# Row factors of two blocks from the transposed input, a ring of its own in the output projection, and later ties for the loads of h

## The chip, the cores and the metric

One core of a Trainium2 chip runs the kernel. TensorE (PE) multiplies matrices, with weight loads listed apart as PEld; VectorE (DVE), ScalarE (ACT) and GpSimd (POOL) work on vectors; SyncE (SP) issues all DMA transfers of this kernel, in the order of its queue. The metric is the device time of one execution in microseconds, as a median of several runs.

## What is computed

One step of a one-layer hybrid encoder over 2048 prompt rows and 32 sample rows of width 1024, all in float32. Cut to what matters here:

```python
def rmsnorm(x, g, eps=EPS):
    xf = x.astype(jnp.float32)
    y = xf * lax.rsqrt(jnp.mean(xf * xf, axis=-1, keepdims=True) + eps)
    return (y * g.astype(jnp.float32)).astype(x.dtype)
...
qa, ka, va, qb, kb, vb = split_proj(rmsnorm(hp, g_attn[i]), w_in[i])
oa = diff_attn_prompt(qa, ka, va, t5_table, lam)
ob = band_attn_prompt(qb, kb, vb, band_table[i])
hp = hp + merge(oa, ob, subln_g[i], out_norm_b[i], w_out[i], lam_init)
...
c = rmsnorm(h, g_mlp)
h = h + jnp.square(jax.nn.relu(c @ w_up)) @ w_down
return h + jax.nn.sigmoid(h @ w_ple_gate) * (p @ w_ple_proj)
```

A row of x (one token) thus gets a factor, 1 / sqrt(mean of its squares + eps), before the projection. A last rmsnorm gives y. Keys and values are outputs too.

## The kernel before

The tokens stand in four blocks of 512 columns (block 1 has the 32 sample rows as well), with features on the partitions: an operand is a tile of 128 partitions by 8 feature groups by 512 tokens. Each float32 operand is split into a high part (rounded, by an ACT copy) and a low part (the rest, by a subtraction on DVE or POOL), and each product is three matmuls: high by high, high by low, low by high (mm3, L267 to L269).

The stages, in the order of the program: preparation and projection of blocks 0 and 1 and their attention; preparation of blocks 2 and 3 (prep, woven with projections of group B); attention of group B; projections of group A for blocks 2 and 3 (proj_a), with onorm of blocks 0 and 1 beside them; the rest of the attention; the output projection of blocks 0 and 1; the MLP of these two; output projection of 2 and 3; then the MLP of blocks 2 and 3 as seven products over half blocks (uphase, dphase); the gates; the end.

A tile framework places the instructions. The program gives each a priority by its place, `tc.high_priority` can raise it ("lifted" does that for the preparation of blocks 2 and 3), and a model of the time (`schedule_with_timeline_sim=True`) then writes each engine's queue. An engine works through its queue in order, and waits with it. A buffer of a pool is given out again once all that read it have run.

What the change and the prediction speak of:

- prep: for each chunk of 256 tokens it loads x twice, as rows (xrows: two tiles of 128 tokens by 1024) and transposed (xcols: xt, one buffer in this stage). ACT squares the rows and sums them (L393), rsqrt makes the factor for 128x2 values, PE transposes it to a row of all partitions (rp, L397), ACT copies it out (rb, L401); then DVE multiplies xt by weight and factor (L405), and ACT and DVE split it into aH and aL (L235, L241).
- weave2 and ONP: while proj_a runs, onorm of block 0 is stepped at its yields 16 and 22, that of block 1 at 17 and 23. A first step loads group B's attention output (oraw), squares and sums it; a second makes the factor and stores it in rB.
- oload(1) and norms(0), beside the output projections of blocks 0 and 1: they load oraw, or tmp from hS, into the ring "tmp" of the pool wk, three buffers, which outproj uses as well for hd and tmp. When the pool is a Mix, oload and outproj load one tile ahead.
- dphase: products 3, 5, 7, 4, 2, 6, 1 in this order, each of 8 chunks (c) of two halves (k). A half needs a split piece of u (dx, four buffers) and of w_down (dw). After a product, DVE adds its result into h. Product 3 adds into block 3's h alone, product 5 into both.
- hstep (L1699 to L1703): in product 3, at chunks 0 to 3, POOL copies one column of dx into each of four h tiles (L1702), and SP then loads these h tiles from hS: the copy ties the load to that place. The h tiles lie where uphase had its temporary tiles.
- gates: the gates of blocks 0 and 1 are woven into dphase; they split their own h (hH, hL) and load w_ple_gate.

Of the kernel before, what the change touches and what calls it, by code (L numbers as in the profile page):

```python
# [12 lines left out]
F32 = mybir.dt.float32  # L13
F32R = mybir.dt.float32r
AF = mybir.ActivationFunctionType
ALU = mybir.AluOpType
# [3 lines left out]
P = 128  # L20
D = 1024
# [9 lines left out]
EPS = 1e-6  # L31
# [13 lines left out]
HALVES = [(0, 1), (2, 3)]  # L45
# [68 lines left out]
OW = 1  # L114
# [1 line left out]
JA0 = [(0, 1), (2, 3, 8)]  # L116
JA1 = [(4, 5), (6, 7)]
JB = [(0, 1), (2, 3, 8), (4, 5), (6, 7)]
ONP = (16, 1, 6)
ONQ = (8, 1, 1)  # L120
PW = 256
GL = 3
# [20 lines left out]
def weave(main, side, step, i=0, n=1):  # L143
    for _ in main:
        if i % step == 0:
            for _ in range(n):
                next(side, None)
        i += 1
    drain(side)
# [47 lines left out]
class Kern:  # L197
# [183 lines left out]

    def prep(self, b, acts, pp, mm, tag, xs=()):
        nc = self.nc
        aH, aL = acts[b]
        xs = list(xs)
        for c0, n in [(0, 256), (256, 256)] + ([(512, SS)] if b == 1 else []):
            m = min(n, P)
            nt = n // m
            x = [xs.pop(0) if xs else self.xrows(b, c0 + P * i, m, pp) for i in range(nt)]
            xt = xs.pop(0) if xs else self.xcols(b, c0, n, pp)  # L390
            st = pp.tile([P, 2], F32, tag="st", name="st")
            for i in range(nt):
                nc.scalar.activation(x[i][:m], x[i][:m], AF.Square, accum_out=st[:m, i : i + 1])  # L393
            r = self.rsqrt(pp, st[:m, :nt], nt, 1.0 / D, EPS, nc.vector, "r1", m)
            rp = mm.tile([P, 512], F32, tag=tag, name="rp")
            for i in range(nt):
                nc.tensor.transpose(rp[:, m * i : m * i + m], r[:, i : i + 1].broadcast_to([m, P]), self.ident[:m, :m])  # L397
            rb = rp
            if b:
                rb = pp.tile([P, 256], F32, tag="rb", name="rb")  # L400
                nc.scalar.activation(rb[:, :n], rp[:, :n], AF.Copy)  # L401
            yield
            for k0 in range(0, 8, 2):
                for k in range(k0, k0 + 2):
                    nc.vector.scalar_tensor_tensor(  # L405
                        xt[:, k, :n], xt[:, k, :n], self.g_attn[:, k : k + 1], rb[:, :n], op0=ALU.mult, op1=ALU.mult
                    )
                sl = (slice(None), slice(k0, k0 + 2))
                self.split(aH[sl + (slice(c0, c0 + n),)], aL[sl + (slice(c0, c0 + n),)], xt[sl + (slice(0, n),)], "act", "dve")
                yield  # L410

    def ktok(self, b):
        if b != 1:
# [782 lines left out]
    def dphase(self, h, pool, md, step):  # L1196
        nc = self.nc
        def wrow(q, c):
            i, j = int(q[0]) - 1, int(q[1]) - 1
            r = pool.tile([P, 2, 512], F32, tag="wd", bufs=6, name="wd")  # L1200
            self.dma(r.rearrange("p a b -> p (a b)"), self.a["w_down"][8 * j + c, i])
            return r

        def operands(m, sq, so, c):
            ws = [wrow(q, c) for q in sq]
            u = self.rawp.tile([P, 2, 512], F32, bufs=self.nraw, name="ut")
            self.dma(u, self.uS[:, m - 1, 2 * c : 2 * c + 2])
# [12 lines left out]
        plan = [  # L1220
            (3, ("11",), add, (("12", add), ("22", add))),
            (5, ("11", "12"), add, (("11", sub), ("12", add))),
            (7, ("12", "22"), sub, (("11", add),)),
            (4, ("22",), add, (("11", add), ("21", add))),
            (2, ("21", "22"), add, (("21", add), ("22", sub))),
            (6, ("21", "11"), sub, (("22", add),)),
            (1, ("11", "22"), add, (("11", add), ("22", add))),
        ]
        for m, sq, so, outs in plan:
            ps = [md.tile([P, 512], F32, tag="mm", name="dp") for _ in range(4)]  # L1230
            for c in range(8):
                for k, (w, x) in enumerate(operands(m, sq, so, c)):
                    if m == 3 and k == 0:
                        step(c, x)
                    for d in range(4):
                        sl = slice(P * d, P * d + P)
                        self.mm3(
                            ps[d], [(w[:, 0, sl], w[:, 1, sl], x[:, 0], x[:, 1])],
                            start=c + k == 0, stop=c == 7 and k == 1,
                        )  # L1240
                if c < 7:
                    yield
            adds = [(d, q, op) for d in range(4) for q, op in outs]
            if m == 1:
                adds.sort(key=lambda x: x[1])
            for d, q, op in adds:
                i, t = int(q[0]) - 1, int(q[1]) - 1
                hv = h[2 + t][4 * i + d]
                nc.vector.tensor_tensor(hv, hv, ps[d], op=op)
            yield  # L1250
# [231 lines left out]
    def run(self):  # L1482
        tc, nc, a = self.tc, self.nc, self.a
        with ExitStack() as top:

            def opened(stack, name, bufs, space=None, side="left"):
                kw = {} if space is None else {"space": space}
                return stack.enter_context(
                    tc.tile_pool(name=name, bufs=bufs, side=side, reuse_waits="tile", **kw)
                )  # L1490
# [7 lines left out]
            mm = opened(psx, "mm", MM, PSUM)  # L1498
# [7 lines left out]
            sg = opened(s12, "sg", 2)  # L1506
            wr = (self.wp, "wr", 3)
            self.rawp = Rings(wr, wr, wr, (opened(s12, "rw", 1), "wr", 1))
            acts = {b: self.actpair() for b in HALVES[0]}
            with ExitStack() as x:  # L1510
                self.nx = 2
                pp = opened(x, "pp0", 3, side="right")
                spare = opened(x, "w4", 1, side="right")
                xs = [self.xrows(0, P * i, P, pp) for i in range(2)]
# [6 lines left out]
                wk = opened(x, "setup", 1, side="right")  # L1521
# [18 lines left out]
            pp = opened(ppx, "pp", 1)  # L1540
# [10 lines left out]
            one, rest = (0,), (1, 2, 3)  # L1551
# [3 lines left out]
            def lifted(gen):  # L1555
                while True:
                    with tc.high_priority(tc.tile_snap_priority() - mark):
                        done = next(gen, self) is self
                    if done:
                        return  # L1560
                    yield

            acts[2] = self.actpair()
            weave(self.proj((1,), 1, acts, sg, mm, vs=(), gs=rest), lifted(self.prep(2, acts, pp, mm, "mm")), 1, 0, 2)
            acts[3] = self.actpair()
            bx = ExitStack()
            bp = opened(bx, "b", 1, side="right")
            for js in JB[: len(JB) // 2]:
                self.attn_b(js, bp, ps_s, ps_t, ps_o)
            prep = lifted(self.prep(3, acts, pp, mm, "mm"))  # L1570
            weave(self.proj((2,), 1, acts, sg, mm, vs=(), gs=rest), prep, 1, 0, 2)
            ppx.close()
            self.vr = Rings(vr)
# [18 lines left out]
            oa = {}  # L1592
# [8 lines left out]
            wk = opened(sq_, "wk", 1)  # L1601
            acc, cn, st = {}, {}, {}
            def norms(b, act, ps):
                r = self.colnorm(acc[b][0], b, 1.0 / D, wk, ps, "mm", None)
                yield
                yield from self.cnorm(b, wk, act, cn, r)

            acc = {b: [] for b in range(4)}
            with ExitStack() as x:
                oq = Sized(opened(x, "oq", 2), BLK, True)  # L1610
                weave(self.outproj(0, wk, oa[0], mm, acc[0]), self.oload(1, wk, oq, oa), 1, 0, OW)
                weave(self.outproj(1, wk, oa[1], mm, acc[1]), norms(0, actq, mm), 1, 1)
            hq = opened(sq_, "hq", 1)
            uq = Sized(opened(sq_, "uq", 10), BLK)
# [7 lines left out]
            def hmove(b, h, load, ds=range(8)):  # L1622
                for d in ds:
                    x, y = h[d][:, : BN[b]], self.hS[:, d, T0[b] : T0[b] + BN[b]]
                    self.dma(*((x, y) if load else (y, x)))
                return h
# [69 lines left out]
            h = {b: hh.tile([P, 8, 512], F32, tag="h", name="h") for b in HALVES[1]}  # L1696
            h = {b: [t[:, d] for d in range(8)] for b, t in h.items()}

            def hstep(c, x):  # L1699
                for b in HALVES[1] if c < 4 else ():  # L1700
                    for d in (2 * c, 2 * c + 1):
                        nc.gpsimd.tensor_copy(h[b][d][:, :1], x[:, 0, :1].bitcast(F32))  # L1702
                    hmove(b, h[b], True, range(2 * c, 2 * c + 2))  # L1703

            fk = opened(top, "fk", 1)
            udx, gqx = ExitStack(), ExitStack()
# [90 lines left out]
```

## Time and profile before

| | |
|---|---|
| median of 3 runs | 2965.36 us (2957.69 to 2965.66) |
| the profiled execution's own time | 2963.89 us |
| its span, first to last instruction | 2962.1 us |
| TensorE's mean granted clock | 0.993 |
| PE busy | 2899.6 us |
| DVE, ACT, POOL busy | 1754.8, 1753.6, 1349.1 us |

In the profile, a row of a group or a timeline gives engine, source line, operation, `out<-in` by the program's names and the shape. "[8.40 <-ACT dx L235]" says that the engine was idle for 8.40 us before the instruction, and that ACT's instruction on dx at line 235 ended it. A row of waits gives the total in us, the number of times and the longest. Lines 235, 241, 220 and 230 belong to helpers, so the tile's name tells where one is. A landing time tells when a DMA's data was there.

### The profile page before, as it was taken

The page shows a single profiled execution, that of the slowest core. Times are in us where ns is not written, and L with a number is a line of the kernel's source. Part 1 is how long each engine was busy: PE and PEld are TensorE (multiplying, and loading weights), DVE is VectorE, ACT ScalarE, POOL GpSimd, SP SyncE. Part 2 cuts the span into 40 slices and gives each one's busy share as a digit, 9 for nine tenths or more (in the row PEclk, how much of TensorE's full clock was granted, in tenths as well). Part 3 has the DMA queues.
Part 4 walks back from the last instruction along what each step waited for, and adds up shares of the span by engine and source line. Part 5 has one row for each costly group of instructions (what it writes and reads, how often), then busy time and mean ns, then how long its engine had stood idle before and what let it go on. Part 6 is the DMA issues. An engine that isn't in the chain of part 4 may idle for free.

```text
span 2962.1 us, 49251 instructions
## 1 busy us (share of the span) xinstructions
PE 2899.6 (98%) x17041; PEld 2560.4 (86%) x17041; DVE 1754.8 (59%) x3930; ACT 1753.6 (59%) x3729; POOL 1349.1 (46%) x1863
## 2 busy tenths in 40 slices
PE   8999999999999999999999999999999989999998
PEld 7899888998889888888899999889788868888886
DVE  6566664444565543565766564447665656766965
ACT  5566666665666665766777675443545445555554
POOL 4675664333355555655455455440855533133000
PEclk9999999999999999999999999999999999999999
DMA  9975578766677544544743433566443495756811
GB/s 347 328 249 198 192 259 271 219 210 207 226 252 225 192 159 157 166 154 151 240 138 123 148 109 120 183 205 199 164 149 139 146 342 191 267 194 202 265 64 57
DMA packets 299785, 578.28 MB, mean 195 GB/s; under 512 B 34672, under 2 KB 132080, under 8 KB 299536
## 3 DMA queue, kind: packets, MB, share of 16 engines
q1 hardware_dynamic: 299536, 575.13, 58.3%
q8 instruction: 135, 2.21, 0.3%
q14 instruction: 114, 0.93, 0.1%
HBM read 443.81 MB, written 131.22 MB: 194 GB/s over the span
## 4 chain that ended last, share of the span: by engine, by line
PE 89%; DMA 5%; DVE 3%; ACT 2%; issue 1%; POOL 1%; SPq 0%; ACTq 0%; DVEq 0%; POOLq 0%
PE s L607 4%; PE ups L269 4%; PE ups L267 4%; PE ups L268 4%; PE dps L267 4%; PE dps L268 4%; PE dps L269 4%; PE qps L267 4%; PE qps L269 4%; PE qps L268 4%; PE xps L269 3%; PE xps L268 3%; PE xps L267 3%; PE dp L267 3%; PE dp L269 3%; PE dp L268 3%
## 5 line engine op out<-in xcount | busy, mean ns | idle before, releaser
L230 POOL TENSOR_TENSOR wl<-wr,wh 128x256 fp32r<-128x256 f32 x888 | 667.8, 783 | 703.2 <-ACT wh L235 583.2
L235 ACT ACTIVATE wh<-wr 128x1024 fp32r<-128x1024 f32 x258 | 272.5, 1056 | 214.4 <-PE dps L268 43.5
L267 PE MATMUL ups<-cH,wh 128*128 128x272 f32 (+1 forms) x768 | 249.9, 326 | 2.3 <-ACT cH L235 1.2
L267 PE MATMUL dps<-uh,wh 128*128 128x272 f32 (+1 forms) x768 | 250.5, 328 | 1.5 <-DVE h L1001 1.1
L269 PE MATMUL ups<-cH,wl 128*128 128x272 f32 (+1 forms) x768 | 249.7, 326 | 0.6 <-DVE wl L241 0.6
L268 PE MATMUL ups<-cL,wh 128*128 128x272 f32 (+1 forms) x768 | 249.6, 325 | 0.0
L268 PE MATMUL dps<-ul,wh 128*128 128x272 f32 (+1 forms) x768 | 248.7, 324 | 0.2 <-DVE ul L241 0.2
L269 PE MATMUL dps<-uh,wl 128*128 128x272 f32 (+1 forms) x768 | 247.9, 324 | 0.0
L267 PE MATMUL qps<-aH,wh 128*128 128x512 f32 (+3 forms) x640 | 228.8, 357 | 6.6 <-DVE qk L487 3.0
L269 PE MATMUL qps<-aH,wl 128*128 128x512 f32 (+3 forms) x640 | 227.4, 355 | 0.0
L268 PE MATMUL qps<-aL,wh 128*128 128x512 f32 (+3 forms) x640 | 226.8, 354 | 0.0
L268 PE MATMUL dp<-dx,dw 128*128 128x512 f32 x448 | 177.9, 397 | 0.0
L267 PE MATMUL dp<-dx,dw 128*128 128x512 f32 x448 | 168.1, 399 | 9.1 <-ACT dx L235 9.1
L269 PE MATMUL dp<-dx,dw 128*128 128x512 f32 x448 | 174.9, 397 | 0.0
L607 PE MATMUL s<-ka,q 128*128 128x512 f32 (+3 forms) x640 | 173.3, 368 | 0.5 <-DVE nm L616 0.4
L788 DVE CUSTOM_DVE_ANT_0 eb<-sb,bb 128x320 f32<-128x320 f32 (+2 forms) x232 | 104.1, 478 | 109.3 <-PE tpb L800 105.0
L613 DVE TENSOR_REDUCE nm<-s 128x1 f32<-128x512 f32 (+1 forms) x192 | 122.1, 641 | 77.8 <-PE s L607 76.0
L267 PEld LDWEIGHTS ups<-cH,wh 128*128 128x128 f32 x768 | 145.2, 189 | 15.2 <-ACT cH L235 1.5
L267 PEld LDWEIGHTS dps<-uh,wh 128*128 128x128 f32 x768 | 144.6, 189 | 14.0 <-DVE h L1001 2.6
L269 PEld LDWEIGHTS ups<-cH,wl 128*128 128x128 f32 x768 | 145.0, 189 | 11.9 <-DVE wl L241 1.0
L268 PEld LDWEIGHTS ups<-cL,wh 128*128 128x128 f32 x768 | 145.3, 189 | 11.6 <-DVE cL L241 0.4
L268 PEld LDWEIGHTS dps<-ul,wh 128*128 128x128 f32 x768 | 144.8, 189 | 10.6 <-DVE ul L241 0.4
(278 smaller groups left out, 8949.4 us busy)
## 6 DMA issues: line engine op xcount, KB each, us to landing
wd<-w_down SPq DMA_DIRECT2D x96, 512.0 KB, 5.2
q<-qS SPq DMA_DIRECT2D x128, 256.0 KB, 4.2
v<-vSa SPq DMA_DIRECT2D x64, 512.0 KB, 3.6
wr<-w_up SPq DMA_DIRECT2D x64, 512.0 KB, 3.8
wr<-w_down SPq DMA_DIRECT2D x64, 512.0 KB, 3.8
ut<-uS SPq DMA_DIRECT2D x56, 512.0 KB, 4.3
wr<-w_qk SPq DMA_DIRECT2D x54, 512.0 KB, 5.2
kS<-qk SPq DMA_DIRECT2D x32, 512.0 KB, 5.4
```

What stands on the lines that cost most here:

```text
L230: nc.gpsimd.tensor_tensor(out[:, sl], a[:, sl], b[:, sl], op=op)
L235: nc.scalar.activation(hi, raw, AF.Copy)
L267: nc.tensor.matmul(ps, lh, rh, start=start and i == 0, stop=False)
L268: nc.tensor.matmul(ps, lh, rl, start=False, stop=False)
L269: nc.tensor.matmul(ps, ll, rh, start=False, stop=stop and i == n - 1)
L607: nc.tensor.matmul(s, q[:, m, hl, P * qi : P * qi + nr], kt[:, m, k0 - kb : k0 - kb + n], start=hl == 0, stop=hl == 1)
L613: nc.vector.tensor_reduce(nmx, s, axis=AX.X, op=ALU.max, negate=True)
L788: nc.vector.tensor_tensor_reduce(e[:, w * i : w * i + w], s, bb[:nr, b0 + w * i : b0 + w * i + w], 1.0, -3e38, ALU.add, ALU.max, st[:, 3 + ...
```

## The change

Blocks 2 and 3 get prepc in place of prep: it loads only xt, squares it on ACT, adds the squares of the eight feature groups on DVE, splits the sum, and lets PE add over the partitions by a product with ones, which leaves the sum in all partitions; rsqrt then works on 128x256 values. The rest of prep is now prows, the same for both. outproj's neighbours, oload(1) and the cnorm of norms(0), get a Mix with a ring of two buffers of their own. ONP moves: the steps of block 0 from yields 16 and 22 to 17 and 24, those of block 1 from 17 and 23 to 23 and 30. hstep is called in every product; it ties and loads block 3's h in product 3 at chunks 4 to 7, two tiles in each, and block 2's in product 5, one in each chunk, and the tie is an ACT copy.

```diff
-ONP = (16, 1, 6)
+ONP = (17, 6, 7)
...
+    def prepc(self, b, acts, pp, mm, tag):
+        nc = self.nc
+        for c0, n in ((0, 256), (256, 256)):
+            xt = self.xcols(b, c0, n, pp)
+            s = pp.tile([P, 256], F32, tag="rs", name="xs")
+            for k in range(0, 8, 2):
+                sq = pp.tile([P, 2, 256], F32, tag="xsq", name="xsq")
+                nc.scalar.activation(sq, xt[:, k : k + 2], AF.Square)
+                if k:
+                    nc.vector.tensor_tensor(s, s, sq[:, 0], op=ALU.add)
+                nc.vector.tensor_tensor(s, s if k else sq[:, 0], sq[:, 1], op=ALU.add)
+            sh = pp.tile([P, 256], F32R, tag="rsh", name="xsh")
+            sl = pp.tile([P, 256], F32R, tag="rb", name="xsl")
+            self.split(sh, sl, s, "act", "dve")
+            rp = mm.tile([P, 512], F32, tag=tag, name="rp")[:, :n]
+            nc.tensor.matmul(rp, self.ones, sh, start=True, stop=False)
+            nc.tensor.matmul(rp, self.ones, sl, start=False, stop=True)
+            rb = self.rsqrt(pp, rp, n, 1.0 / D, EPS, nc.vector, ("rs", "rb"), P, None, 256)
+            yield
+            yield from self.prows(c0, n, acts[b], xt, rb)
...
-                    if m == 3 and k == 0:
-                        step(c, x)
+                    if k == 0:
+                        step(m, c, x)
...
-            weave(self.proj((1,), 1, acts, sg, mm, vs=(), gs=rest), lifted(self.prep(2, acts, pp, mm, "mm")), 1, 0, 2)
+            weave(self.proj((1,), 1, acts, sg, mm, vs=(), gs=rest), lifted(self.prepc(2, acts, pp, mm, "mm")), 1, 0, 2)
...
-            prep = lifted(self.prep(3, acts, pp, mm, "mm"))
+            prep = lifted(self.prepc(3, acts, pp, mm, "mm"))
...
-                yield from self.cnorm(b, wk, act, cn, r)
+                yield from self.cnorm(b, wo, act, cn, r)
...
-                weave(self.outproj(0, wk, oa[0], mm, acc[0]), self.oload(1, wk, oq, oa), 1, 0, OW)
+                wo = Mix(wk, tmp=(opened(x, "ot", 1), 2))
+                weave(self.outproj(0, wk, oa[0], mm, acc[0]), self.oload(1, wo, oq, oa), 1, 0, OW)
...
-            def hstep(c, x):
-                for b in HALVES[1] if c < 4 else ():
-                    for d in (2 * c, 2 * c + 1):
-                        nc.gpsimd.tensor_copy(h[b][d][:, :1], x[:, 0, :1].bitcast(F32))
-                    hmove(b, h[b], True, range(2 * c, 2 * c + 2))
+            def hstep(m, c, x):
+                b, ds = {3: (3, range(2 * c - 8, 2 * c - 6) if c > 3 else ()), 5: (2, (c,))}.get(m, (2, ()))
+                for d in ds:
+                    nc.scalar.activation(h[b][d][:, :1], x[:, 0, :1].bitcast(F32), AF.Copy)
+                hmove(b, h[b], True, ds)
```

More of the change, by code (lines that the diff above doesn't have):

```diff
@@ L383, in prep @@
         nc = self.nc
-        aH, aL = acts[b]
         xs = list(xs)
@@ L402, in prep, with prows @@
             yield
[L403 to L410, printed above, removed]
+            yield from self.prows(c0, n, acts[b], xt, rb)
[18 more added lines that the diff above has]
+            yield
+            yield from self.prows(c0, n, acts[b], xt, rb)
+    def prows(self, c0, n, act, xt, rb):
+        for k0 in range(0, 8, 2):
+            for k in range(k0, k0 + 2):
+                self.nc.vector.scalar_tensor_tensor(
+                    xt[:, k, :n], xt[:, k, :n], self.g_attn[:, k : k + 1], rb[:, :n], op0=ALU.mult, op1=ALU.mult
+                )
+            sl = (slice(None), slice(k0, k0 + 2), slice(c0, c0 + n))
+            self.split(act[0][sl], act[1][sl], xt[:, k0 : k0 + 2, :n], "act", "dve")
+            yield
     def ktok(self, b):
```

## The prediction

> **What bounds the kernel now.** I read the page's first part, then who ended TensorE's (PE's) waits, then the timeline around the longest of those waits, and last the stretches that the diff touches.
>
> ```profile
> span 2962.1 us, 49251 instructions
> ## 1 busy us (share of the span) xinstructions
> PE 2899.6 (98%) x17041; PEld 2560.4 (86%) x17041; DVE 1754.8 (59%) x3930; ACT 1753.6 (59%) x3729; POOL 1349.1 (46%) x1863
> ```
>
> PE is busy for 98% of the span. The change hardly touches PE's own work, so what it can win is PE's idle time, 2962.1 − 2899.6 = 62.5 us with the head and the tail of the span, and the slow clock after idle time. VectorE (DVE), ScalarE (ACT) and GpSimd (POOL) are half idle: an instruction added to them costs only where PE waits for it. The waits of PE, each row with total, number and longest:
>
> ```profile
> PE dp L267 <- ACT dx L235: 9.1, 2, 8.4
> PE rp L397 <- DVE rsy L282: 6.2, 1, 6.2
> PE gps L267 <- ACT wh L235: 3.8, 1, 3.8
> PE tpp L682 <- DVE e L646: 3.2, 2, 2.3
> PE qps L267 <- DVE qk L487: 3.0, 2, 2.2
> PE sb L785 <- DVE stb L788: 2.5, 3, 1.3
> ...
> PE ups L267 <- ACT cH L235: 1.2, 1, 1.2
> ```
>
> The first and the third row, 9.1 and 3.8 us, lie at the start of the down phase, where the diff moves the h loads. The second lies at the kernel's start and is not touched. The others are small and scattered. Next, the two long waits from the timelines of POOL, PE and ACT:
>
> ```profile
> 2404.08 7.98 POOL L220 TENSOR_TENSOR hL<-h,hH 128x256 fp32r<-128x256 f32 x7
> 2412.00 1.82 POOL L1702 COPY h<-dx 128x1 f32<-128x1 f32 x11
> 2404.92 0.40 PE L269 MATMUL dp<-dx,dw 128*128 128x512 f32 x1
> 2413.71 0.80 PE L267 MATMUL dp<-dx,dw 128*128 128x512 f32 x1 [8.40 <-ACT dx L235]
> 2413.03 1.15 ACT L235 ACTIVATE dx<-ut 128x512 fp32r<-128x512 f32 x2 [6.16 <-POOL h L1702]
> ```
>
> This is one knot. The tie in hstep (L1702) copies a column of dx into h, so that the loads of h come behind it. It reads dx, so it holds one of the four dx buffers until it has run. It stands on POOL behind eight hL pieces, the last seven of which take 7.98 us. By the fourth chunk of product 3 all four buffers are held, ACT can't write the next dx, and PE is idle for 8.40 us. The third row's wait, 3.8 us, follows from the same ties (below).
>
> **Ties and h loads (hstep, dphase).** The ties go from POOL to ACT. Block 3's eight loads go to chunks 4 to 7 of product 3, two in each; block 2's eight go to product 5, one in each chunk. So no dx is held in chunks 0 to 3, and later ones are held by an instruction on the engine that has just written that dx. The 8.40 us and the 0.7 us before it (9.1 in all) go. What follows now:
>
> ```profile
> L211 SPq DMA_DIRECT2D h<-hS x16: 319/350/946, 2413.5 to 2424.6; - x16
> 2425.92 0.52 SPq L211 DMA_DIRECT2D wr<-w_ple_gate  x1
> 2431.99 1.06 ACT L235 ACTIVATE wh<-wr 128x1024 fp32r<-128x1024 f32 x1 [0.64 <-DMA wr<-w_ple_gate]
> 2433.09 0.51 PE L267 MATMUL gps<-hH,wh 128*128 128x512 f32 x1 [3.76 <-ACT wh L235]
> ```
>
> All 16 loads of h stand in SP's queue from 2413.5 to 2424.6, the gate's weight is issued behind them at 2425.92, and PE waits 3.76 us for it. With the 16 loads spread over two products the weight is issued some 11 us earlier, against a wait of 3.8: it goes too. The granted clock adds to both waits. Windows from the end of each, and one of the output projection (window, length, PE busy, clock):
>
> ```profile
> 366.00:400.00 34.00, 28.63 (x224) 1.00 0.57 192
> 886.20:892.00 5.80, 5.68 (x29) 0.71 0.54 214
> 2413.70:2418.00 4.30, 4.29 (x13) 0.66 1.03 396
> 2433.00:2438.00 5.00, 4.91 (x14) 0.66 0.66 206
> ```
>
> After the 8.40 us the clock is 0.66 over 4.3 us, which loses 4.3 × 0.34 = 1.5 us; after the 3.76 us it loses 5.0 × 0.34 = 1.7. So the knot costs 9.1 + 3.8 + 1.5 + 1.7 = 16.1 us.
>
> New there are 16 one-column copies on ACT. The nearest row is POOL's, 1.82 us for 11: 16 × 0.17 = 2.7 us, beside PE's work. A tie that waits on ACT keeps back all that is queued behind it: the next dx and dw, and so PE. It can wait for the h space, which the last stores of uS leave:
>
> ```profile
> 2402.96 6.40 DMA uS<-u
> ```
>
> That ends at 2409.4. Chunk 4's dx, two chunks ahead of PE, is due about then or later, so I take no wait. If ACT did stand there, the bound is 2409.4 − 2404.9 = 4.5 us. The DVE also has hL and dv to do in these microseconds, and may hand over a dx late. I take 14.5 of the 16.1 us, and keep 16.1 and 8 as ends.
>
> **Row factors of blocks 2 and 3 (prepc).** Removed are eight loads of 512 KB, eight squares of 128x1024 on ACT and eight transposes. Each of the four chunks of 256 columns gets four ACT squares of 128x512, seven DVE adds of 128x256, a split, two ones-matmuls and rsqrt on 128x256 in place of 128x2. From this stage, grouped by shape (count, busy us, mean ns):
>
> ```profile
> L405 DVE SCALAR_TENSOR_TENSOR xt<-xt,columns,rb 128x256 f32<-128x256 f32 x32 | 18.7, 652 | 0.0
> ...
> L241 DVE TENSOR_TENSOR aL<-xt,aH 128x512 fp32r<-128x512 f32 x16 | 10.4, 677 | 0.0
> L235 ACT ACTIVATE aH<-xt 128x512 fp32r<-128x512 f32 x16 | 9.1, 621 | 8.6 <-DVE xt L405 8.6
> ...
> L393 ACT ACTIVATE x<-x 128x1024 f32<-128x1024 f32 x2 | 2.1, 1059 | 0.8 <-DMA x<-x_prompt 0.8
> ...
> L397 PE MATMUL rp<-ident,rsy 128*128 128x128 f32 x8 | 1.6, 279 | 0.0
> ...
> L277 ACT ACTIVATE rsy<-rsv 128x256 f32<-128x256 f32 x2 | 0.8, 409 | 0.0
> ```
>
> PE: eight transposes of 0.28 us (1.6 us of union) against eight short matmuls: zero within 1 us. ACT: 4 × 0.62 + 4 × 0.41 in, 2 × 1.06 and small ones out: a wash. DVE: 12 operations of 128x256 more in a chunk, each 0.34 us (half of aL's 0.677 for half the elements) to 0.65 (L405): 4.1 to 7.8 us.
>
> What matters is latency. Before, the factors came from separately loaded rows and were ready ahead of xt. Now they start when xt has landed: squares 2.5 us with the adds running behind, two last adds 0.7 to 1.3, split 0.4 + 0.5, matmuls 0.5, three ACT steps 1.2, four DVE steps 1.4 to 2.6, so 7 to 9 us. xt has a single buffer, so a chunk's load waits for the chunk before it: nothing hides this but the slack until PE needs the operands.
>
> ```profile
> 398.78 0.69 DVE L241 TENSOR_TENSOR aL<-xt,aH 128x512 fp32r<-128x512 f32 x1
> 411.75 0.40 PE L267 MATMUL qps<-aH,wh 128*128 128x512 f32 x1
> 440.69 2.47 DVE L241 TENSOR_TENSOR aL<-xt,aH 128x512 fp32r<-128x512 f32 x4
> 465.36 0.39 ACT L486 ACTIVATE qk<-qps 128x256 fp32r<-128x256 f32 x1
> ```
>
> Block 2's operands end at 399.5 and PE takes them up at 411.75: 12 us of slack. Block 3's end at 443.2; its first product is copied out at 465.36 and began between 5 and 9.6 us before (24 matmuls of 0.40 us that overlap): 13 to 17 us of slack. Block 2's first chunk can have its factors done before the operand buffers come free, so one chunk's 7 to 9 us fall into 12, and two chunks' 14 to 18 into 13 to 17. It just fits, or just fails to. But PE's queue is in order, and a ones-matmul that waits for twelve DVE operations, where a transpose waited for four tiny ones, can hold up products behind it. The window 366 to 400 already has 34 − 28.6 = 5.4 us of idle PE. Bounds: all of it gone (−5), or as much again (+5) and a slow clock (+1.7). I take +1.5, nearer to the middle since the loads get fewer.
>
> The Trainium skill, page "SBUF — State Buffer", section "Who interferes with whom", states that a DVE instruction with two SBUF inputs and a GpSimd instruction that reads SBUF exclude each other, the later one waiting out the whole instruction. It speaks against this change, because all the new adds have two SBUF inputs. L405 agrees: 652 ns for half the elements that aL does in 677.
>
> **Own ring (wo) and onorm (ONP).** In the output projection of blocks 0 and 1, oraw, hd, tmp and the cnorm loads shared three buffers. Now oload and cnorm have two of their own and oload runs one load ahead. What of PE's waits belongs here is at most: part of sb L785 (1.3, before the window at 886.2), its clock 5.8 × 0.29 = 1.7, ups L267 1.2, and some 2 us of single waits under 1 us: about 6. SP shows the coupling, a load of hd that waits for the buffer's store:
>
> ```profile
> SPq L211 <- DMA hS<-hd: 15.3, 12, 3.5
> ```
>
> I take −3 and keep 0 and −6. ONP moves both onorm steps by 1 to 7 yields of 35, each before the end of that loop; DVE, ACT and POOL do the same work there: 0 within 1.
>
> The Trainium skill, "TensorE: Matmul & The Clock Gate", Part 1, has the clock halve after at least one idle window of about 3.4 us. By it the 1.7 us at 886.2 would not exist, since the wait there is 1.3 us, and this part would be worth 4.5 at most; the row differs (0.71), and the row decides.
>
> **Sum.** −14.5 + 1.5 − 3 = −16.0 us against the profiled execution's own 2963.89 (span 2962.1 and 1.8 around it): 2947.9. That execution is 1.5 below the median 2965.36, so as a median 2949. Any change below 0.3%, 8.9 us, I call the same: a measurement of this kernel can hardly tell it.
>
> **Rivals.**
> A, the knot is only loosened: the ties stand on ACT until the stores of uS have landed (4.5 us and 1.5 of clock), and the hL burst delays dx for 2 more. For it: all of that work is due at 2402 to 2412. Against it: with no dx held, ACT can run four dx ahead. Then −8 + 1.5 − 3 + 1.5: 2956, chance 0.13.
> B, slower: the ones-matmuls stand in PE's queue where the transposes stood, and each of the four waits out the chain. At 8.5 us and 1.7 of clock each that is +41, against −17.5: 2987. For it: PE in order, DVE at its POOL-slowed pace. Against it: the slack, and attention work to fill. It decides sign only above (17.5 + 8.9) / 4 = 6.6 us per chunk; I give it 0.06. By the SBUF page's rule all twelve operations would go at the slow pace; that is this rival, not the forecast.
> C, the spread h loads collide with w_down and uS streams in products 3 and 5 and the adds into h come late: a load is some 6 us from issue to landing, so +6: 2955, chance 0.05. Against it: products last 45 us or more and the loads stand a chunk or more ahead.
> D, the change does not do what it says: engine orders are written by the kernel's own scheduling model, which may lay the down phase out anew and put a like wait elsewhere: 2964, chance 0.06.
>
> **Numbers.** The forecast has 0.70. Its own range is 2938 (16.1, −5 and −6) to 2957. With A and C, which end at 2955 to 2956, and part of D the range is 2937 to 2960. Faster: 0.66 of the forecast's 0.70, 0.05 of A, 0.02 of C: 0.73. Same: 0.04 + 0.08 + 0.03 + 0.05 of D: 0.20. Slower: B's 0.06 and 0.01 of D: 0.07.
>
> **What would show it.** Right: no wait of PE for dx above 1 us in the down phase, no drop of the clock after 2400, h loads in two loose trains, gps not waiting. PE's idle in the window of preparation within 3 us of 5.4, the ones-matmuls without waits of their own. Wrong: a dx wait with ACT's h tie as its end (A), PE waiting for the ones-matmul's operand or for the first product of block 2 or 3 (B), DVE's adds into h ended by DMA (C), or busy PE above 2900 us.

## The result and the profile after

The changed kernel takes 2949.9 us (median of 5 runs, 2947.66 to 2953.32), the kernel before 2963.11 in the same session: a ratio of 0.9957, 95% interval 0.9943 to 0.9972. The profiled execution took 2947.66 us, its span is 2945.7 us. The forecast was 2949. The total is right; the terms behind it are not all right, and that is what the rest is about.

The first part of the page of the kernel after:

```profile
span 2945.7 us, 49285 instructions
## 1 busy us (share of the span) xinstructions
PE 2894.4 (98%) x17041; PEld 2560.2 (87%) x17041; DVE 1779.5 (60%) x3962; ACT 1756.8 (60%) x3745; POOL 1356.7 (46%) x1847
```

PE's idle time is 2945.7 − 2894.4 = 51.3 us, against 62.5 before. Who ended PE's waits, after:

```profile
PE ss L730 <- DVE sh L237: 6.5, 1, 6.5
PE rp L396 <- DVE rsy L282: 5.9, 1, 5.9
PE qps L267 <- DVE qk L510: 5.2, 2, 3.7
```

The rows "dp <- dx" (9.1) and "gps <- wh" (3.8) are gone. New at the top is a wait of 6.5 us for the high part of attention A's sum (sh), and the wait for qk has grown from 3.0 to 5.2. Both lie between 370 and 410 us, where blocks 2 and 3 are prepared. To see where the time went, take the stretches one by one. Each row has the window, its length, the busy time of PE, PEld, DVE, ACT and POOL, the granted clock, the DMA share and GB/s. Before:

```profile
0.00:130.00 130.00, 114.32 (x699) 101.09 (x700) 70.05 (x167) 70.71 (x152) 69.38 (x97) 0.97 0.98 344
360.00:480.00 120.00, 113.91 (x717) 101.81 (x715) 72.08 (x223) 76.19 (x187) 69.13 (x100) 1.00 0.77 255
700.00:1000.00 300.00, 293.08 (x1736) 258.08 (x1735) 161.34 (x508) 197.98 (x388) 137.32 (x190) 0.99 0.70 228
2380.00:2475.00 95.00, 82.13 (x337) 65.16 (x336) 59.85 (x83) 44.49 (x76) 33.09 (x46) 0.95 0.83 299
```

After:

```profile
0.00:130.00 130.00, 116.77 (x743) 104.97 (x744) 81.16 (x196) 72.54 (x161) 74.87 (x102) 1.00 0.97 333
360.00:480.00 120.00, 101.60 (x586) 89.66 (x585) 89.03 (x227) 70.96 (x176) 59.32 (x79) 0.90 0.62 207
700.00:1000.00 300.00, 297.24 (x1820) 264.67 (x1819) 163.03 (x521) 198.84 (x390) 139.12 (x189) 1.00 0.72 236
2380.00:2475.00 95.00, 95.00 (x409) 76.71 (x408) 69.84 (x101) 54.80 (x105) 34.18 (x37) 1.00 0.88 328
```

What PE loses in a window is its length minus PE busy times clock. (The clock is a mean over the window, idle time included, so a window with a low clock reads one or two us too high; and it is printed with two digits, which is 0.6 us either way in 120 us.) By this the down phase (2380 to 2475) goes from 17.0 to 0, the preparation (360 to 480) from 6.1 to 28.6, the start from 19.1 to 13.2, and 700 to 1000 from 9.9 to 2.8. One term is as forecast, one is many times its size, and one gain was not in the forecast at all.

### The profile page after: what moved, and what is told of

The parts are those of the page before. It is cut to its first block, busy times and chain, and to the rows that moved or that the text cites. A ratio compares the mean times of both kernels' runs of the same rounds, so it can differ in the third digit from the quotient of the medians.

```text
span 2945.7 us, 49285 instructions
## 1 busy us (share of the span) xinstructions
PE 2894.4 (98%) x17041; PEld 2560.2 (87%) x17041; DVE 1779.5 (60%) x3962; ACT 1756.8 (60%) x3745; POOL 1356.7 (46%) x1847
## 4 chain that ended last, share of the span: by engine, by line
PE 92%; DVE 3%; DMA 2%; ACT 1%; issue 1%; POOL 1%; SPq 0%; ACTq 0%; DVEq 0%; POOLq 0%
PE ups L268 4%; PE dps L267 4%; PE ups L269 4%; PE ups L267 4%; PE dps L269 4%; PE dps L268 4%; PE s L630 4%; PE qps L267 4%; PE qps L268 4%; PE dp L267 4%; PE qps L269 4%; PE dp L268 4%; PE dp L269 4%; PE xps L269 3%; PE xps L268 3%; PE xps L267 3%
## 5 line engine op out<-in xcount | busy, mean ns | idle before, releaser
L230 POOL TENSOR_TENSOR wl<-wr,wh 128x256 fp32r<-128x256 f32 x888 | 679.1, 795 | 702.4 <-ACT wh L235 622.0
L267 PEld LDWEIGHTS dps<-uh,wh 128*128 128x128 f32 x768 | 144.3, 188 | 15.6 <-DVE h L1024 4.1
L268 PEld LDWEIGHTS ups<-cL,wh 128*128 128x128 f32 x768 | 144.7, 188 | 11.2
L267 PEld LDWEIGHTS ups<-cH,wh 128*128 128x128 f32 x768 | 144.7, 188 | 11.1
L268 PEld LDWEIGHTS dps<-ul,wh 128*128 128x128 f32 x768 | 144.6, 188 | 11.2
L269 PEld LDWEIGHTS ups<-cH,wl 128*128 128x128 f32 x768 | 144.5, 188 | 11.1
```

The lines of the kernel that those rows point to most:

```text
L230: nc.gpsimd.tensor_tensor(out[:, sl], a[:, sl], b[:, sl], op=op)
L267: nc.tensor.matmul(ps, lh, rh, start=start and i == 0, stop=False)
L268: nc.tensor.matmul(ps, lh, rl, start=False, stop=False)
L269: nc.tensor.matmul(ps, ll, rh, start=False, stop=stop and i == n - 1)
```

## The experiments

The first theory after the result: each part acts in its own stage, and the preparation gives back what the ties win. Its rival: the scheduling model lays the program out anew for any edit, so that the parts can't be told apart (D of the prediction). Twelve kernels; ratios are to runs of the kernel before in the same session (medians 2958.42 to 2963.11). Each row of losses comes from one trace. "Start" is PE's idle time from 0 to 130 us; the other columns are losses by the formula above.

| kernel | median, us | ratio, 95% interval | start | 360–480 | 700–1000 | 2380–2475 |
|---|---|---|---|---|---|---|
| before | 2958–2963 | | 15.7 | 6.1 | 9.9 | 17.0 |
| after | 2949.90 | 0.9943–0.9972 | 13.2 | 28.6 | 2.8 | 0 |
| ties_only | 2940.21 | 0.9919–0.9955 | 15.7 | 5.8 | 8.4 | 0 |
| rows_only | 2975.58 | 1.0038–1.0068 | 13.6 | 30.9 | 7.3 | 17.6 |
| ring_only | 2953.88 | 0.9971–0.9992 | 15.2 | 7.9 | 3.1 | 17.4 |
| no_rows | 2939.15 | 0.9915–0.9944 | 15.6 | 5.6 | 5.0 | 0 |
| xsq_halves | 2950.97 | 0.9957–0.9980 | 12.9 | 31.4 | 2.5 | 0 |
| one_pair | 2937.69 | 0.9907–0.9937 | 11.1 | 16.0 | 2.6 | 0 |
| no_factor | 2930.38 | 0.9874–0.9935 | 12.0 | 6.6 | 3.0 | 0 |
| ties_early_act | 2968.55 | 1.0018–1.0038 | 14.2 | 28.5 | 2.8 | 18.7 |
| ties_late_pool | 2948.49 | 0.9951–0.9974 | 13.4 | 31.0 | 2.8 | 0 |
| no_rows_latemark | 2936.79 | 0.9905–0.9935 | 16.0 | 7.1 | 3.1 | 0 |
| rows_tied | 2951.08 | 0.9954–0.9983 | 14.1 | 14.1 | 2.0 | 0 |
| rows_mid | 2938.98 | 0.9908–0.9935 | 11.2 | 10.7 | 3.7 | 0 |

### One part alone, and all but one

ties_only is the kernel before with the new hstep and its calls in dphase; rows_only has prepc alone; ring_only has the new ring and ONP alone; no_rows is the changed kernel with the old preparation:

```diff
-lifted(self.prepc(2, acts, pp, mm, "mm"))
+lifted(self.prep(2, acts, pp, mm, "mm"))
...
-prep = lifted(self.prepc(3, acts, pp, mm, "mm"))
+prep = lifted(self.prep(3, acts, pp, mm, "mm"))
```

> Before, with the new ties and nothing else (ACT copies, block 3's h in product 3 at chunks 4 to 7, block 2's in product 5). Theory: the parts work each in its own stage, and the ties alone are worth the 16 us that the stage 2384 to 2460 lost before (12.8 idle, 3.2 of slow clock) and no longer loses: 2947 against 2963, with the preparation (366 to 443) at its old 6 us of idle PE. Rival, the layout: any edit makes the time model write all queues anew, so gains and losses turn up in stages that the edit doesn't touch; then the ratio differs from this by 5 us or more either way.

> Before, with prepc for blocks 2 and 3 and nothing else (old ties on POOL, old ring, old ONP). Theory: the factors' chain is exposed on PE, and the stage 360 to 470 loses 27 us in place of 6 as in the changed kernel; the start (0 to 360), which lost 6 us less in the changed kernel, does so here too because the rows' loads are gone: +21 - 6 = +15, 2978. If the start's gain isn't the rows', 2984. Rival (my forecast's bound for this part): at most +7, 2970, the loss at 360 to 470 being an effect of the other edits on the layout.

> Before, with the own ring of two buffers and the moved ONP and nothing else. Theory: the stage 800 to 1000 lost 9.6 us before and 2.7 after, which is this edit's: -7, 2956; 2384 to 2460 and 360 to 470 stay as before. Rival, the layout: that stage's gain came from rows or ties; then it stays near 2963, the stage losing over 7 us.

> The changed kernel with the old prep for blocks 2 and 3: ties, ring and ONP new, rows loaded as before. Theory: the 21 us that 360 to 470 loses more goes, and the start's 6 us come back: 2950 - 21 + 6 = 2935, faster than both. If the start's gain isn't the rows', 2929. Rival: the row factors cost at most 7 us, and the rest of that stage's loss is layout: 2943 or above.

Measured against 2959.42 in that session: ties −19.2, rows +16.2, ring −5.5. In the table each part shows in its own column: the ties empty the last one, the ring takes the fourth to about 3, the rows raise the third. no_rows has the third back at 5.6 and the start back at 15.6, and nothing like the knot of before stands elsewhere. So D falls as an account of the whole.

The times add up only roughly. The three parts give −8.5 together, where the changed kernel had −13.2 in its session (interval −16.9 to −8.3). The rows cost 16.2 us on the kernel before, but 7.1 on top of no_rows (−20.3 against −13.2, each in its own session); the ring gives 5.5 alone, but 1.1 on top of the ties (2940.21 to 2939.15). And no_rows' time lies between its theory (2935) and its rival (2943 or above): its columns decide for the theory, its time doesn't. ring_only holds the new ring and the moved ONP, and no run separates these two.

### Why the preparation loses 22 us

In the profile after, the second chunk of block 2. The first square on ACT:

```profile
381.86 0.63 ACT L411 ACTIVATE xsq<-xt 128x512 f32<-128x512 f32 x1 [0.97 <-DMA xt<-xT]
```

DVE from there:

```profile
382.52 0.43 DVE L414 TENSOR_TENSOR xs<-xsq 128x256 f32<-128x256 f32 x1 [0.84 <-ACT xsq L411]
383.64 0.43 DVE L413 TENSOR_TENSOR xs<-xs,xsq 128x256 f32<-128x256 f32 x1 [0.69 <-ACT xsq L411]
...
387.94 0.68 DVE L413 TENSOR_TENSOR xs<-xs,xsq 128x256 f32<-128x256 f32 x1 [0.76 <-ACT xsq L411]
388.66 0.42 DVE L414 TENSOR_TENSOR xs<-xs,xsq 128x256 f32<-128x256 f32 x1
389.00 0.29 DVE L237 CAST sh<-sq 128x256 fp32r<-128x256 f32 x1
389.56 0.81 DVE L241 TENSOR_TENSOR xsl<-xs,xsh 128x256 fp32r<-128x256 f32 x1 [0.28 <-ACT xsh L235]
395.79 0.43 DVE L279 TENSOR_TENSOR rsv<-rsv,rsy 128x256 f32<-128x256 f32 x1 [5.42 <-ACT rsy L278]
...
398.15 6.41 DVE L428 SCALAR_TENSOR_TENSOR xt<-xt,columns,rsy 128x256 f32<-128x256 f32 x8
```

and PE beside it:

```profile
389.44 0.55 PE L730 MATMUL ss<-sh,ones_r 128*128 128x256 f32 x1 [6.46 <-DVE sh L237]
389.79 0.41 PE L419 MATMUL rp<-xsh,ones_r 128*128 128x256 f32 x1
...
393.87 0.28 PE L420 MATMUL rp<-xsl,ones_r 128*128 128x256 f32 x1
```

The sum is split at 390.4, 8.5 us after the first square's start, where the prediction had 4.1 to 4.7. Two things lie across this stage. The first is PE's wait of 6.46 us. The product that PE's queue has next is attention A's, with the high part of its own sum (sh), and has nothing to do with block 2. Its operand passes through ACT (os), POOL (its square, sq) and DVE (the cast to sh), and stands behind other work on all three. ACT and then POOL:

```profile
382.98 0.63 ACT L411 ACTIVATE xsq<-xt 128x512 f32<-128x512 f32 x1 [0.49 <-DVE xs L414]
383.52 1.04 ACT L235 ACTIVATE wh<-wr 128x1024 fp32r<-128x1024 f32 x1
...
385.32 0.38 ACT L723 ACTIVATE os<-o 128x256 f32<-128x256 f32 x1
384.63 3.14 POOL L230 TENSOR_TENSOR wl<-wr,wh 128x256 fp32r<-128x256 f32 x4 [4.08 <-ACT wh L235]
387.73 0.61 POOL L725 TENSOR_TENSOR sq<-os 128x256 f32<-128x256 f32 x1
```

os starts 2.35 us after PE's last product of o has ended (382.97), behind a square, the split of a weight (wh) and another square. sq starts 2.03 us after os has ended, behind four low parts of that weight (wl), for whose high part POOL had stood idle 4.08 us. The cast starts 0.66 us after sq has ended, behind the last two adds. These delays are 5.0 of the 6.46 us, and DVE's adds are the smallest of them; the chain's own work is 1.4. In the kernel before the same chain lost 0.9 us on POOL and next to nothing elsewhere, and PE had other products until 385.26:

```profile
381.30 0.38 ACT L700 ACTIVATE os<-o 128x256 f32<-128x256 f32 x1 [1.25 <-PE o L698]
382.57 0.61 POOL L702 TENSOR_TENSOR sq<-os 128x256 f32<-128x256 f32 x1
383.21 0.29 DVE L237 CAST sh<-sq 128x256 fp32r<-128x256 f32 x1 [1.03 <-POOL sq L702]
385.26 0.28 PE L707 MATMUL ss<-sh,ones_r 128*128 128x256 f32 x1
```

How much of the delay is the squares' own time on ACT, and how much the new order in which the queues were written, no run separates.

The second thing: the low part of the new sum reaches PE only at 393.87, behind products already queued, so the roots begin at 394.2 and the scaling at 398.15: 16 us from square to scaling, not 7 to 9. The next long wait of PE, 3.70 us until 408.5, is for a copy of the projection beside it (qk), which DVE runs at 408.04, behind the scaling and the low parts aL. For the operands of blocks 2 and 3 themselves (aH, aL) PE waits nowhere between 360 and 480 us.

The adds also wait for squares (0.84, 0.69, 0.76), since xsq has a single buffer. That was the next theory.

**xsq_halves.**

```diff
-            for k in range(0, 8, 2):
-                sq = pp.tile([P, 2, 256], F32, tag="xsq", name="xsq")
-                nc.scalar.activation(sq, xt[:, k : k + 2], AF.Square)
-                if k:
-                    nc.vector.tensor_tensor(s, s, sq[:, 0], op=ALU.add)
-                nc.vector.tensor_tensor(s, s if k else sq[:, 0], sq[:, 1], op=ALU.add)
+            prev = None
+            for k in range(8):
+                sq = pp.tile([P, 256], F32, tag="xsq", bufs=2, name="xsq")
+                nc.scalar.activation(sq, xt[:, k], AF.Square)
+                if k:
+                    nc.vector.tensor_tensor(s, s if k > 1 else prev, sq, op=ALU.add)
+                prev = sq
```

> The changed kernel, with the squares of the new preparation in two buffers of half the size (eight squares of 128x256 and seven adds per chunk, the same memory). Theory (the sum of squares is a ping-pong through one buffer: ScalarE waits for VectorE's adds and VectorE for ScalarE's next squares, and TensorE stands behind the chain): from the first square to the factor takes about 11 us per chunk in place of 16 and 24, and TensorE's loss between 360 and 480 us falls from 27.5 to about 15 us; 2938 us. Rival (the loss comes from the order on VectorE and from the single buffer of the transposed x, not from the ping-pong): chain and loss stay within 4 us of what they were, 2946 to 2950 us.

The theory fell: 2950.97 us and 31.4 of loss. The same chunk on DVE:

```profile
387.17 0.45 DVE L414 TENSOR_TENSOR xs<-xs,xsq 128x256 f32<-128x256 f32 x1
...
387.72 3.88 DVE L414 TENSOR_TENSOR xs<-xs,xsq 128x256 f32<-128x256 f32 x5
...
392.09 0.42 DVE L241 TENSOR_TENSOR xsl<-xs,xsh 128x256 fp32r<-128x256 f32 x1
```

and PE's longest wait there:

```profile
PE rp L420 <- DVE sh L237: 8.2, 1, 8.2
```

Five adds now run back to back, in 3.88 us, and PE still waits 8.2, but for another product: here it is the ones-matmul itself. Its operand xsh, which is split after the last add, is ready at 392.06, and PE goes on at 392.11; the cast that the row names ended at 392.09. The ping-pong went and the chain of serial adds stayed. Is the chain the cost, then, or what follows it?

**one_pair** sums one pair of squares in place of four (`for k in (0,)`); **no_factor** forms no factor at all:

```diff
-            s = pp.tile([P, 256], F32, tag="rs", name="xs")
...
-            rb = self.rsqrt(pp, rp, n, 1.0 / D, EPS, nc.vector, ("rs", "rb"), P, None, 256)
+            rb = pp.tile([P, 256], F32, tag="rb", name="rb")
+            nc.scalar.activation(rb, xt[:, 0], AF.Copy)
```

> The changed kernel, which sums only the first two of the eight squares of each chunk (six squares and six adds per chunk are left out, so the row factors are not the true ones); ones-matmuls, Newton steps and loads stay. Theory (the length of the chain of squares and adds is what TensorE waits for in the preparation): the loss between 360 and 480 us falls from 27.5 to 6 to 10 us, 2930 to 2934 us. Rival (that the sum is formed there at all costs it: two matmuls in TensorE's queue behind VectorE, the Newton steps, and x held until they are done): at least 18 us of the loss stay, 2940 us or more.

> The changed kernel without any forming of the row factors in the new preparation: squares, adds, splits, ones-matmuls and Newton steps are left out, and in place of the factors stands a copy of one row of x (so the rows are scaled wrongly); the loads of x transposed, the scaling and the splits into high and low parts stay. Theory (all of the loss above the kernel before comes from the factors being formed there: about 11.5 us of it from the length of the sum, the remaining 10 us from the matmuls and Newton steps behind it): the loss between 360 and 480 us is 6 us or less, and the start keeps its 6 us; 2928 to 2932 us. Rival (the remaining 10 us come from something else, the single buffer of x transposed or the layout of memory): the loss stays at 12 us or more, 2935 us or more.

The window 360 to 480 of one_pair, and then of no_factor:

```profile
360.00:480.00 120.00, 108.36 (x646) 96.48 (x645) 77.92 (x221) 73.23 (x178) 67.04 (x90) 0.96 0.69 236
```

```profile
360.00:480.00 120.00, 114.53 (x682) 101.70 (x681) 61.91 (x187) 69.58 (x163) 74.08 (x104) 0.99 0.77 253
```

Losses of 16.0 and 6.6 us. With one_pair I had 6 to 10 or 18 and more; it came between. So of the 22 us, about 12 are the length of the sum (squares and adds), about 9 are the rest of forming the factor there (products, roots, and waiting for them), and none is left when the factor costs nothing. The 9 are not divided further: in one_pair PE's waits are 2.8 us for the high part of the sum and 5.3 for loads of q, which the other kernels don't have in that size.

### Place or engine of the ties

ties_early_act puts all 16 ties back at chunks 0 to 3 of product 3, on ACT; ties_late_pool leaves them at the new places, on POOL:

```diff
-                    nc.scalar.activation(h[b][d][:, :1], x[:, 0, :1].bitcast(F32), AF.Copy)
+                    nc.gpsimd.tensor_copy(h[b][d][:, :1], x[:, 0, :1].bitcast(F32))
```

> The changed kernel with all 16 ties and h loads back in the first four chunks of product 3, but the ties still on ScalarE. Theory (the place decides: x of four chunks is held by ties that wait for h's memory, and the 16 loads stand in one train): the wait for dx of about 9 us comes back and with it most of the 16 us, 2962 to 2966 us. Rival (the engine decides: it was GpSimd's copies that came late): the 16 us stay won, 2948 to 2951 us.

> The changed kernel with the ties at their new places (products 3 and 5, in two loose trains) but on GpSimd again. Theory (the place decides): the 16 us stay won, 2948 to 2952 us. Rival (the engine matters too, since GpSimd is behind with its own work there and its ties hold x): a wait for dx of 3 us or more comes back, 2953 to 2960 us.

The place decides. With ACT at the old place the knot is back, 18.7 us and 2968.55, a little more than the theory's 2962 to 2966; with POOL at the new place the column stays 0 and the time is 2948.49, the changed kernel's within its interval. PE's waits of ties_early_act and its ACT queue:

```profile
PE dp L267 <- ACT dx L235: 7.0, 2, 6.2
...
PE gps L267 <- ACT wh L235: 6.0, 1, 6.0
```

```profile
2413.94 1.60 ACT L1727 ACTIVATE h<-dx 128x1 f32<-128x1 f32 x16 [2.50 <-DMA pn<-pT]
2415.45 1.66 ACT L235 ACTIVATE dx<-ut 128x512 fp32r<-128x512 f32 x3
```

All 16 ties run at 2413.94 here; on POOL before they began at 2412.00. In the changed kernel the first four run here:

```profile
2411.48 0.48 ACT L1726 ACTIVATE h<-dx 128x1 f32<-128x1 f32 x4 [2.79 <-DMA uS<-u]
...
2414.70 1.06 ACT L235 ACTIVATE wh<-wr 128x1024 fp32r<-128x1024 f32 x1 [1.94 <-DMA wr<-w_ple_gate]
```

This stage lies some 4 us later in the trace of ties_early_act, so count from the issue of uS's last store, which leaves h's memory: 2402.96 before, 2407.05 in ties_early_act, 2404.90 in the changed kernel. The first tie runs 9.0 us after it on POOL, 6.9 and 6.6 on ACT. On ACT both rows name a DMA as the end of ACT's idle time, 2.50 and 2.79 us, once the stores of uS. On POOL the store had landed at 2409.36, and the ties came 2.6 us later, when the hL pieces were done.

So POOL's queue of hL pieces, on which the prediction laid weight, was the smaller part of the knot: PE's longest wait for dx is 6.2 us on ACT in place of 8.4. The total doesn't show even that, as the wait for the gate's weight grew from 3.8 to 6.0. A tie that comes early in product 3 waits for h's memory on either engine and holds its dx. Whether the load of pn or another release freed the ties in ties_early_act the row can't settle, since it names only the last event.

### The start

In the trace of before, row loads of blocks 2 and 3, 512 KB each, run in the first 130 us, where the DMA share is 0.98. The kernels with these loads there have 15.2 to 16.0 us of PE's idle time in that window, all others 11.1 to 14.2. By the loss formula, in which the expectations below count, the two groups overlap: 16.3 to 21.4 against 11.2 to 18.7. One wait of the kernel before, at 46.7 us, belongs to the difference:

```profile
PE qps L267 <- ACT wh L235: 2.4, 1, 2.4
```

This wait, 2.1 to 2.4 us, stands in the five kernels with these loads in the first 130 us and in rows_tied, which keeps the first two of them there, and in no other; at its place the others have 0 to 1.8 us. Can one keep the old preparation and move these loads? Three tries:

no_rows_latemark lets the priority of the preparation count from a later place:

```diff
-            mark = tc.tile_snap_priority()
...
+                mark = None
                 for js in JA0:
...
                     self.attn_a(js, pool, ps_s, ps_t, ps_o)
+                    mark = mark or tc.tile_snap_priority()
```

> The changed kernel with the old preparation (row loads and transposed factors), whose priority counts from the end of the first group of the first attention instead of from its begin, so that the eight row loads and their squares cannot run in the first 130 us. Theory (the 6 us that the new preparation wins at the start come from these loads leaving a stage whose DMA engines are full): the start's loss falls from 19.9 to 13 to 14 us and the preparation stays at 6 us; 2933 us, the fastest of all. Rival (the start's loss hangs on the layout of memory or on chance): 2939 us as with the old preparation; or the later row loads come too late for the factors, TensorE waits between 360 and 480 us, 2945 us.

The row loads stayed where they were, so the edit did not do what it was meant to, and its start of 16.0 says nothing on the theory. Its 2936.79 is the lowest median of a kernel that computes everything, but by the intervals it can't be told from no_rows and rows_mid.

rows_tied lets row loads wait for the scaled x of the chunk before, rows_mid holds the first of them until the end of the first attention group:

```diff
         x = pp.tile([P, D], F32, tag="x", bufs=self.nx ** 2, name="x")
+        if late is not None:
+            self.nc.scalar.activation(x[:, :1], late[:, 0, :1], AF.Copy)
```

> The changed kernel with the old preparation, in which the row loads of blocks 2 and 3 (all but the first chunk's two) wait by a one-column copy for the scaled x of the chunk before, so that they run from about 375 us on and not in the first 130 us. Theory (the start's 6 us come from row loads leaving a stage whose DMA engines are full): the start's loss falls from 19.9 to 13 to 15 us, the preparation stays within 2 us of 5.6 us; 2932 to 2935 us. Rival (the start's loss is not the row loads'): 2937 to 2940 us as with the old preparation. Second rival (the later rows make TensorE wait in the preparation): its loss rises over 10 us, 2942 us or more.

> The changed kernel with the old preparation, in which the first of the eight row loads of blocks 2 and 3 waits by a one-column copy for the end of the first attention's first group (about 173 us); the others follow it through the one buffer of x, so that none runs in the first 130 us and the factors of the first chunks are still formed long before 375 us. Theory (row loads in the full stage at the start cost about 4 us, as the kernels with and without them differ there by 18.9 to 14.7 us on average, and rows that come before 375 us make nobody wait): the start's loss is 14 to 16 us, the preparation's 5 to 7 us; 2933 to 2936 us, the fastest of the correct kernels. Rival (the start does not gain by it, or the rows collide with attention): 2937 us or more.

rows_tied: the second rival; the late rows cost more in the preparation (14.1) than the start won. By the loss formula its start is 18.7, not the theory's 13 to 15. rows_mid, three windows:

```profile
0.00:130.00 130.00, 118.81 (x762) 107.99 (x763) 72.85 (x183) 69.66 (x151) 76.63 (x105) 1.00 0.96 331
130.00:360.00 230.00, 226.34 (x1603) 212.25 (x1602) 150.74 (x443) 161.44 (x453) 143.98 (x224) 0.99 0.68 227
360.00:480.00 120.00, 112.65 (x685) 100.86 (x685) 70.32 (x209) 73.37 (x180) 69.17 (x100) 0.97 0.75 244
```

and two waits of its second window:

```profile
ACT x L394 <- DMA x<-x_prompt: 11.0, 6, 4.9
...
PE qps L267 <- DVE qk L512: 3.1, 1, 3.1
```

The start's loss falls to 11.2, so the row loads in all likelihood did cost the start some us; it is one trace, and kernels without these loads reach 11.2 to 18.7. But the squares now stand in ACT's queue and wait for each load, 11.0 us over six, with the work of projection and attention behind them: 5.9 us are lost there, where other kernels have 0 to 3, and 10.7 in the preparation. The sum is no better than no_rows: 2938.98 against 2939.15.

## Why the prediction was right in the sum and wrong in a term

- **The knot, −14.5 (ends 8 and 16.1): right.** 17.0 us of loss became 0. Ties moved alone give −19.2 as medians. The dx and gps rows are gone, and the clock is 1.00 in the down phase, as "what would show it" had it. Rival A's wait did occur, 2.79 us of ACT for the stores of uS, against the bound of 4.5; PE was busy throughout, so it cost nothing. The reason was wrong in one point: most of the wait was for h's memory and not for POOL's hL pieces, so moving the ties to another engine alone wins nothing.
- **Row factors, +1.5 (bounds −5 to +6.7): the term that was mis-sized.** It measured +22 in its stage, far above the upper bound. The step that failed is "so 7 to 9 us": it added up the instructions as if the engines stood ready. From square to scaling it was 16 us in this chunk: 8.5 to the split sum (forecast 4.1 to 4.7), 3.8 until PE had both parts (0.5), 4.0 for the roots (2.6 to 3.8). The second failure is "nothing hides this but the slack until PE needs the operands". That slack held: PE waited nowhere in this stage for aH or aL. What PE waited for was other work that passed the same queues, first of all attention A's sum, 6.46 us, which had no slack.
- **Rival B**, with a chance of 0.06, had the stage and nearly the price: 10.2 us per chunk by four chunks. What came was half of that, and below the 6.6 us per chunk from which it would have decided the sign. Its mechanism, PE standing for the ones-matmul's operand, cost only 0.6 us in the changed kernel; it came in xsq_halves, with 8.2 us.
- **Own ring, −3 (0 to −6): in its range.** Without it 700 to 1000 loses 7.3 to 9.9 us, with it 2.0 to 5.0; with the moved ONP it gives −5.5 alone and −1.1 on top of the ties.
- **The start, not in the forecast:** I priced the eight row loads as a wash for ACT and PE, and never asked in which stage they run. They ran early, in the fullest one. PE's idle time there fell from 15.7 to 13.2, the loss from 19.1 to 13.2; how much of the latter is the loads' and how much the clock's scatter from kernel to kernel, the runs leave open.
- **The rest.** −17.0 + 22.5 − 5.9 − 7.1 = −7.5, while the span fell by 16.4. Of the 9 us between, 4 are idle time of PE outside these windows, in single waits. The others are clock, and what the formula can't resolve. They differ from kernel to kernel where the code is the same; no run assigns them.

So +22 in place of +1.5 was made up by gains at the start, in the ring's stage and in scattered places. The total was right by luck. No rival's time came out. Of the signs to look for, the ones-matmuls without waits failed, by 0.6 us. PE's idle time "within 3 us of 5.4" held in the window it was taken from, 366 to 400, with 8.3 us, and told nothing: over the whole stage, 360 to 480, it went from 6.1 to 18.4.

Two slips in the numbers decided nothing. The forecast was moved to the median by 1.5 us, and A's 2956 and B's 2987 were not. And the forecast's upper end, 2957, is not the sum of its upper ends: −8 + 6.7 + 0 gives 2964 as a median.

## What to carry to other kernels

Price a new serial chain by what stands behind it in each queue that it passes, not by its own operands' slack: the longest wait here was for a foreign sum that was late on ACT, on POOL and on DVE, 5.0 us in all. Follow such a wait back through every engine before naming one: the row names DVE, which had 0.66 of it. For a tie or any held buffer, ask first when its target's memory comes free; the engine that executes it is the lesser question. And of a load that is dropped or moved, look up in which stage it really runs: these row loads ran in the first 130 us, for a stage that begins near 360.

## What the runs showed of the hardware

The same eight DVE operations took 6.41 us in the changed kernel (at 398.15, above), with POOL busy for 6.48 of the 7 us from 398 to 405, and in one_pair, with POOL busy for 2.14 of 4.5 us:

```profile
391.15 3.70 DVE L426 SCALAR_TENSOR_TENSOR xt<-xt,columns,rsy 128x256 f32<-128x256 f32 x8
```

That is 0.80 against 0.46 us each. The Trainium skill, page "SBUF — State Buffer", section "Who interferes with whom", has such DVE operations and GpSimd's reads exclude each other; the two rows agree. The prediction's own sign of it, 652 against 677 ns, compared two kinds of operation that both have two SBUF inputs, and shows less. Its bound for one DVE operation of 128x256, 0.34 to 0.65 us, was passed in this chunk. It isn't the pace of all chunks: in the changed kernel's next one, from 428.65 on, the eight took 3.26 us, 0.41 each, with POOL idle.

The wait of 6.46 us also had its clock. Windows of the changed kernel:

```profile
383.00:386.50 3.50, 0.00 (x0) 0.00 (x0) 2.41 (x8) 2.83 (x8) 1.86 (x3) 1.00 0.99 329
386.50:389.40 2.90, 0.00 (x0) 0.00 (x0) 2.00 (x5) 0.91 (x2) 1.88 (x4) 0.50 0.77 258
389.40:393.30 3.90, 3.87 (x17) 3.90 (x18) 0.81 (x1) 0.13 (x1) 0.70 (x1) 0.50 0.29 108
393.30:397.00 3.70, 3.70 (x32) 3.70 (x30) 1.17 (x4) 2.17 (x7) 0.51 (x1) 1.00 0.02 4
```

The clock falls to 0.50 about 3.5 us into the wait and stays there for 3.9 us after PE has work again: 17 products in 3.90 us, then 32 in 3.70. A wait of 6.5 us thus costs some 8.4.
